# Latent attention heads in pairs, and the row minima of the next unit between the score tiles

## The chip, the cores and the metric

The kernel runs on one core of a Trainium2 chip. The metric is the device time of one execution in microseconds; the time of a kernel is the median of its runs. The engines are TensorE (PE, with its weight loads listed as PEld), VectorE (DVE), ScalarE (ACT), GpSimd (POOL) and SyncE (SP, which issues the DMAs).

## The reference

One layer of a hybrid encoder, 1024 tokens of width 1024, all in float32. The part that the change touches is the multi-head latent attention; beside it runs a banded attention of eight heads, and an output projection and a gated MLP with a short convolution follow.

```python
h = modulate(rmsnorm(x, g_attn_norm), sh_a, sc_a)
q_lat, kv_lat, k_rope, ca_qkv = split(h @ w_in)
q  = (rmsnorm(q_lat) @ w_q_up)  -> (S, 8 heads, 96)
kv = (rmsnorm(kv_lat) @ w_kv_up) -> k_nope (64), v (64) per head
k  = concat(k_nope, broadcast(k_rope))             # 96 per head
q, k = rmsnorm per head, rotary on the last 32
s = q k^T * 96**-0.5, masked: key chunk <= query chunk (chunks of 64)
o_mla = softmax(s) v
o_ca  = banded attention of 8 more heads
x = x + g_a * (concat(o_mla, o_ca) @ w_out)
x = x + g_m * (silu(gate) * val @ w_down)          # gate, val: conv of h @ w_up
```

## The kernel before, in words

The kernel is written as a sequence of operations on tiles of named pools; a planner at build time takes that sequence and fixes the order of each engine's queue from its own estimates. `tc.high_priority(offset=n)` moves a block's operations n places ahead in the planner's ranking (`OFF_S` = 400 for scores, `OFF_V` = 200 for values). `tc.issue_after(ins)` lets the block's operations on that engine stand only behind `ins`. A pool tag with `bufs=n` has n buffers; a new tile of that tag waits until the oldest one's readers are done. At run time each engine takes its queue in order.

Large matrix products are split into a high and a low half (fp32r), three matmuls for one.

The latent attention works in units: a unit (`Latent`) is one head and one group `g` of 512 queries; `gr` is the group of four heads, `hh` the head in it. Keys stand on partitions in the score tiles (scores transposed), queries along the columns. A unit of `g` = 0 has four key blocks and two score tiles, one of `g` = 1 has eight key blocks and four score tiles; the four blocks on the diagonal are shortened and masked by a memset. The steps of a unit:

- `prep`: two pages, `Q` and `K`, are made by `qk_page` (L612 and on): four transposes on TensorE into a PSUM buffer of tag `T` (one buffer, `TB` = 1), a copy to the high half on ScalarE (L619 for queries, L622 for keys), a difference to the low half on VectorE (L620, L623).
- `rows_min` (L724 to L738): for four tiles of 128 queries a one-pass product of high halves (`sm`, L732) in a score slot, a mask (L734), the minimum over the keys on VectorE (`mm`, L736), and its transpose into one row (`mtm`, L737, tag `T`). ScalarE copies the negated row into row 96 of the query page (L738), so that the score product subtracts it by itself. (Keys carry the negative scale, so the minimum is what a maximum usually is.)
- `scores(x)`: one tile `st` with up to two pieces of 512 columns (three matmuls each, L751 to L753), masks (L755), exponentials on ScalarE (`pm`, L761).
- `values(x)`: products of these with the values (`pvm`, L779). The value operand holds 64 columns of values and 64 of ones, so one half of the accumulator's partitions holds the output and the other half the sums; which half is which alternates with `hh`. After the last tile ScalarE copies the sums across (`om`, L787), VectorE takes the reciprocal (L788) and the product (L789), and SP stores 64 rows of `oT_d` (L790).

Both `sm` and `st` live in the PSUM tag `S`, which has two slots of two banks; the accumulator `pv` has one buffer.

The order: for each of the 16 units, in the order head by head with `g` = 0 then 1, `begin(next unit)` (its needs, `prep` and all of `rows_min`) comes ahead of this unit's score tiles, and the values lag two score tiles behind. `pace` puts in filler work: after each step it takes pieces from a list of generators (projections for later heads, then `f_up(0)` and `f_up(1)`, the up-projections of the two groups of four latent heads, then `f_oca`, the output projection of the banded heads) worth `R_MLA` = 0.5 times the step's cost. `need(key)` forces a generator to its end; a unit needs `up1` if `gr` or `g` is 1, otherwise `up0`. The tag `pg` (`pgtile`, six buffers of the size of a page) holds the transposed latents until `f_up(1)` has read them. Before the latent units the banded heads run in tiles (`Unit`, with scores in L656), and the first latent unit is begun at their end. After them the output projection of the latent heads (`op`) reads `oT_d` back by token tiles.

Of the kernel before, what the change touches and what calls it, by code (L numbers as in the profile page):

```python
# [12 lines left out]
F32 = mybir.dt.float32  # L13
F32R = mybir.dt.float32r
# [3 lines left out]
AF = mybir.ActivationFunctionType  # L18
ALU = mybir.AluOpType
AX = mybir.AxisListType  # L20
PSUM = bass.MemoryType.PSUM
MUL, ADD, SUB, MIN, MAX = ALU.mult, ALU.add, ALU.subtract, ALU.min, ALU.max

P = 128
D = 1024
S = 1024
# [5 lines left out]
BIG = 1e30  # L32
QR, KVR, ROPE, NOPE, VD = 256, 128, 32, 64, 64
QK = NOPE + ROPE
# [5 lines left out]
OFF_S, OFF_P, OFF_V = 400, 200, 200  # L40
# [22 lines left out]
def layer_kernel(ctx, tc, I, out):  # L63
    nc = tc.nc
    pe, act, dve, pool, sp = nc.tensor, nc.scalar, nc.vector, nc.gpsimd, nc.sync
# [18 lines left out]
    cst = ctx.enter_context(tc.tile_pool(name="cst", bufs=1))  # L84
    dram = ctx.enter_context(tc.tile_pool(name="dram", bufs=1, space=bass.MemoryType.DRAM))
    oT_d = dram.tile([ND, P, S], F32, name="oT_d")
# [9 lines left out]
    ident = cst.tile([P, P], F32, name="ident")  # L96
# [11 lines left out]
    gk_m = cst.tile([P, 1], F32, name="gk_m")  # L108
# [22 lines left out]
    ps = psA.__enter__()  # L131
# [12 lines left out]
    def pgtile(shape, dt, name):  # L144
        return apg.tile(shape, dt, name=name, tag="pg", bufs=6)
# [11 lines left out]
    trail = []  # L157
# [79 lines left out]
    for d in range(ND):  # L237
        if d + 1 < ND:
            load_ada(d + 1)
        w = wada[d]  # L240
# [91 lines left out]
    at = att.__enter__()  # L332
# [279 lines left out]
    def qk_page(src, name, rows, tag, bufs, gain, top=None):  # L612

        pt = ps.tile([P, 512], F32, name=f"{name}_ps", tag="T", bufs=TB)
        for j in range(4):
            pe.transpose(pt[:top or rows, j * P:(j + 1) * P], src(j), ident[:])
        pg = at.tile([P, 2, 512], F32R, name=name, tag=tag, bufs=bufs)
        if gain is None:
            act.activation(pg[:rows, 0], pt[:rows], AF.Copy)  # L619
            dve.tensor_tensor(pg[:rows, 1], pt[:rows], f32(pg[:rows, 0]), op=SUB)  # L620
        else:
            act.activation(pg[:top or rows, 0], pt[:top or rows], AF.Copy, scale=gain[:top or rows])  # L622
            dve.scalar_tensor_tensor(pg[:rows, 1], pt[:rows], gain[:rows], f32(pg[:rows, 0]), op0=MUL, op1=SUB)  # L623
        return pg

    class Unit:
# [58 lines left out]
        def values(u, i):  # L685
            if i % 4 == 0:
                u.pv = ps.tile([P, 512], F32, name=f"pv{u.nm}_{u.g}", tag="pv", bufs=1)
            c = slice((i % 4) * P, (i % 4 + 1) * P)
            tt, lo, nk = u.pt[i]
            todo = [(lo + j, tt[:, h * nk + j, :]) for j in range(nk) for h in range(2)]  # L690
            with tc.high_priority(offset=OFF_V):
                for x, (j, mov) in enumerate(todo):
                    last = pe.matmul(u.pv[:, c], u.vst(j), mov, start=(x == 0), stop=(x == len(todo) - 1))
                trail.append(last.ins)
                if i % 4 == 3:
                    dst = at.tile([P, 512], F32, name=f"o{u.nm}_{u.g}", tag="o", bufs=1)
                    r0, r1 = (slice(64, 128), slice(0, 64)) if u.odd else (slice(0, 64), slice(64, 128))
                    inv = vscale[u.vs][1]
                    act.activation(dst[r0], u.pv[r1], AF.Copy, scale=inv[r1])
                    dve.scalar_tensor_tensor(dst[r0], u.pv[r0], inv[r0], dst[r0], op0=MUL, op1=ADD)  # L700
                    sp.dma_start(u.dst_d[r0, u.g * 512:(u.g + 1) * 512], dst[r0])
            return 56 * len(todo)

    class Latent:


        def __init__(u, gr, hh, g):
            u.gr, u.hh, u.g, u.nm = gr, hh, g, f"m{gr}{hh}"
            u.need = ["up1"] if gr or g else ["up0"]
            d = [[(4 * g, 0)], [(4 * g + 1, 128), (4 * g + 3, 384)], [(4 * g + 2, 256)]]  # L710
            u.pieces = [[(kb, 0)] for kb in range(4 * g)] + d
            u.pr = {}

        def prep(u):
            gr, hh, g = u.gr, u.hh, u.g
            u.q = qk_page(lambda j: mq[gr, (4 * g + j) // 2][:, j % 2, hh, 0:QK], f"mq{gr}{hh}_{g}", QK, "Q", 2, None)
            k = qk_page(lambda j: mk[gr, (4 * g + j) // 2][:, j % 2, hh, :], f"mk{gr}{hh}_{g}", QK, "K", 3, gk_m[:],
                        QK + 1)
            pages[gr, hh, g] = k
            u.k = [pages[gr, hh, i] for i in range(g + 1)]  # L720

        def rows_min(u):

            with tc.high_priority(offset=OFF_S):  # L724
                mt = ps.tile([P, 512], F32, name=f"mt{u.nm}_{u.g}", tag="T", bufs=TB)
                for j in range(4):
                    n = (4 * u.g + j + 1) * P
                    nm = f"{u.nm}_{4 * u.g + j}"
                    s = ps.tile([P, 1024], F32, name=f"s{nm}", tag="S", bufs=2)
                    for c in range(0, n, 512):  # L730
                        w = min(512, n - c)
                        pe.matmul(s[:, c:c + w], u.q[:QK, 0, j * P:(j + 1) * P], u.k[c // 512][:QK, 0, :w],  # L732
                                  start=True, stop=True)
                    dve.memset(s[0:64, n - 64:n], BIG)  # L734
                    m = cst.tile([P, 1], F32, name=f"m{nm}", tag="m", bufs=4)
                    dve.tensor_reduce(m[:], s[:, :n], axis=AX.X, op=MIN)  # L736
                    last = pe.transpose(mt[0:1, j * P:(j + 1) * P], m[:], ident[:])  # L737
                act.activation(u.q[QK:QK + 1, 0], mt[0:1], AF.Copy, scale=-1.0)  # L738

        def scores(u, x):  # L740
# [25 lines left out]
        def values(u, x):  # L766
            if x == 0:
                u.pv = ps.tile([P, 512], F32, name=f"pv{u.nm}_{u.g}", tag="pv", bufs=1)
            cost = 0
            with tc.high_priority(offset=OFF_V):  # L770
                for y in (2 * x, 2 * x + 1):
                    if y >= len(u.pieces):
                        break
                    o = 0
                    for kb, c in u.pieces[y]:
                        w = 512 - c
                        o2 = u.hh % 2
                        v = mv[u.gr, kb][:, u.hh // 2, o2:o2 + 2, :].rearrange("p a b -> p (a b)")
                        last = pe.matmul(u.pv[:, c:], v, u.pr[y][:, o:o + w], start=(kb == 0),  # L779
                                         stop=(y == len(u.pieces) - 1))  # L780
                        o += w
                        cost += 4 * w / 2.4
                trail.append(last.ins)
                if 2 * x + 2 >= len(u.pieces):
                    dst = at.tile([P, 512], F32, name=f"o{u.nm}_{u.g}", tag="o", bufs=1)
                    r0, r1 = (slice(64, 128), slice(0, 64)) if u.hh % 2 else (slice(0, 64), slice(64, 128))
                    act.activation(dst[r0], u.pv[r1], AF.Copy)  # L787
                    dve.reciprocal(dst[r0], dst[r0])  # L788
                    dve.tensor_tensor(dst[r0], u.pv[r0], dst[r0], op=MUL)  # L789
                    sp.dma_start(oT_d[2 * u.gr + u.hh // 2][r0, u.g * 512:(u.g + 1) * 512], dst[r0])  # L790
            return cost

    biases = {}
# [59 lines left out]
    def pace(cost, ratio):  # L853
        debt[0] += cost * ratio
        while debt[0] > 0:
            c = fill_step()
            if c is None:
                debt[0] = 0.0
                return
            debt[0] -= c  # L860

    units = [ca_unit(p, g, o) for p in range(4) for g in range(2) for o in range(2)]
    lat = [Latent(gr, hh, g) for gr in range(2) for hh in range(4) for g in range(2)]

    def begin(u):
        need(u.need)
        u.prep()
        u.rows_min()

    tiles = [(u, i) for u in units for i in range(4 * u.g, 4 * u.g + 4)]  # L870
    for n in range(len(tiles) + DEPTH):
        if n < len(tiles):
            u, i = tiles[n]
            if i % 4 == 0:
                need(u.need)
                u.prep()
            pace(u.scores(i), R_CA)
        elif n == len(tiles):
            begin(lat[0])
        if n >= DEPTH:  # L880
            u, i = tiles[n - DEPTH]
            if i % 4 == 0:
                need(u.needv)
            pace(u.values(i), R_CA)
    wait = []
    for n, u in enumerate(lat):
        if n + 1 < len(lat):
            begin(lat[n + 1])
        for x in range(2 + 2 * u.g):
            pace(u.scores(x), R_MLA)  # L890
            wait.append((u, x))
            if len(wait) > 2:
                v, y = wait.pop(0)
                pace(v.values(y), R_MLA)
    for v, y in wait:
        v.values(y)
    need(["oca"])
# [322 lines left out]
```

## Time and profile before

| | us |
|---|---|
| median of 3 runs | 1573.38 (1569.08 to 1576.13) |
| the profiled execution | 1573.6 |
| its span, first to last instruction | 1571.8 |
| mean granted TensorE clock over the span | 0.917 |
| TensorE busy | 1366.2 (87% of the span) |
| VectorE busy | 1006.2 (64%) |
| ScalarE busy | 605.0 (38%) |
| GpSimd busy | 703.4 (45%) |

Busy time counts instructions of the engine itself; a busy TensorE is not TensorE at its peak, since the ends of pipelined matmuls are modelled and the granted clock can be below one. In the groups of instructions a row reads: line, engine, operation, output and input tiles, shapes and count, then busy time and mean duration in ns, then the idle time of that engine just ahead of these instructions and what ended most of it. A row of waits reads: the waiting engine and operation, the one that released it, total time, times, the longest. In the order of time a row gives start, duration, engine, line, operation, and in brackets the idle time ahead and its releaser. The span is also given in forty equal slices, each digit the busy share of a slice in tenths.

### The profile page before, as it was taken

What the parts mean: (1) busy time and instruction counts of PE and PEld (TensorE: products, weight loads), DVE (VectorE), ACT (ScalarE), POOL (GpSimd) and SP (SyncE); (2) the same over time, 40 slices, a digit from 0 to 9 for tenths busy, and PEclk for the clock granted to TensorE, in tenths of its full rate; (3) what the DMA queues carried; (4) which work ended last, traced back from release to release, by engine and by line L of the source; (5) the groups of instructions that cost most, each with busy time, mean ns of one, the idle gap of its engine ahead of it and who ended that gap; (6) DMA issues with size and microseconds to landing.
All of it is one profiled execution on the core that took longest, in us unless ns stands there. A gap on an engine that the chain in (4) does not pass through costs nothing.

```text
span 1571.8 us, 19114 instructions
## 1 busy us (share of the span) xinstructions
PE 1366.2 (87%) x6608; PEld 1090.8 (69%) x6608; DVE 1006.2 (64%) x1660; ACT 605.0 (38%) x1146; POOL 703.4 (45%) x643
## 2 busy tenths in 40 slices
PE   3869989998779787776789599999999999999997
PEld 2759868877546455544457488878788887787885
DVE  6865776665886334444346787777877777556653
ACT  5544443343554322223325443334444443333331
POOL 5264552564445000001037265556656664565662
PEclk9979969997888878778789699999999999999999
DMA  7323566454303100011173132232222234446542
GB/s 265 132 73 89 116 134 140 118 123 102 81 15 101 44 26 29 20 34 58 34 261 134 41 107 107 99 103 94 82 80 81 84 112 141 160 144 212 172 153 95
DMA packets 137821, 164.89 MB, mean 105 GB/s; under 512 B 71414, under 2 KB 102266, under 8 KB 136700
## 3 DMA queue, kind: packets, MB, share of 16 engines
q1 hardware_dynamic: 137724, 163.67, 34.5%
q8 instruction: 52, 0.85, 0.2%
q14 instruction: 45, 0.37, 0.1%
HBM read 119.07 MB, written 28.84 MB: 94 GB/s over the span
## 4 chain that ended last, share of the span: by engine, by line
PE 55%; DVE 15%; DMA 12%; POOL 8%; issue 6%; ACT 3%; SPq 1%; DVEq 0%; POOLq 0%; ACTq 0%
PE p L992 8%; PE p L994 8%; PE p L993 8%; PE pvm L779 4%; POOL wds L82 4%; DMA aw<-w_ada 4%; PE sc L656 3%; PE dnp L1135 2%; PE dnp L1137 2%; PE dnp L1136 2%; DVE om L788 2%; PE stm L751 2%; PE stm L752 1%; PE stm L753 1%; DVE adacc L244 1%
## 5 line engine op out<-in xcount | busy, mean ns | idle before, releaser
L82 POOL TENSOR_TENSOR wds<-wd,wds 128x512 fp32r<-128x512 f32 x88 | 152.7, 1755 | 102.2 <-ACT wds L75 102.2
L82 POOL TENSOR_TENSOR wc<-ws,wc 128x512 fp32r<-128x512 f32 x22 | 65.3, 2970 | 129.3 <-ACT wc L75 129.3
L1137 PE MATMUL dnp<-wds,g 128*128 128x512 f32 x308 | 119.4, 394 | 3.6 <-DVE g L82 3.6
L1135 PE MATMUL dnp<-wds,g 128*128 128x512 f32 x308 | 120.0, 392 | 1.7 <-DVE xo L1143 1.7
L1136 PE MATMUL dnp<-wds,g 128*128 128x512 f32 x308 | 120.4, 392 | 0.0
L1125 DVE TENSOR_TENSOR wd<-wd,gmbc 128x1024 f32<-128x1024 f32 x44 | 65.0, 1478 | 86.2 <-DMA wd<-w_down 86.2
L75 ACT ACTIVATE wds<-wd 128x512 fp32r<-128x512 f32 x88 | 54.8, 624 | 160.2 <-PE dnp L1137 152.6
L761 ACT ACTIVATE pm<-stm 128x512 f32<-128x512 f32 (+1 forms) x80 | 43.6, 551 | 123.6 <-DVE stm L755 67.2
L779 PE MATMUL pvm<-pm,vt 128*128 128x512 f32 (+1 forms) x192 | 80.6, 544 | 6.3 <-ACT pm L761 6.0
L755 DVE MEMSET stm<- 64x64 f32 x64 | 7.1, 112 | 120.9 <-PE stm L753 105.6
L71 POOL TENSOR_SCALAR hlc<-Pc,ric 128x640 f16<-128x640 f32 (+2 forms) x64 | 45.7, 716 | 81.2 <-DVE ric L676 41.4
L788 DVE RECIPROCAL om<-om 64x512 f32<-64x512 f32 x16 | 53.6, 3347 | 44.3 <-ACT om L787 44.2
L1069 DVE SCALAR_TENSOR_TENSOR u<-c,pk,u 128x1023 f32<-128x1023 f32 x44 | 77.6, 1769 | 1.8 <-ACT u L1068 1.8
L82 POOL TENSOR_TENSOR cl<-cl,ch 128x512 fp32r<-128x512 f32 x8 | 10.4, 1302 | 150.5 <-ACT ch L75 149.3
L82 DVE TENSOR_TENSOR g<-gr,g 128x512 fp32r<-128x512 f32 x44 | 70.4, 1602 | 11.4 <-ACT g L75 11.4
L656 PE MATMUL sc<-k,q 64*128 64x512 f32 (+3 forms) x288 | 70.5, 373 | 7.4 <-ACT Pc L673 5.5
L673 ACT ACTIVATE Pc<-sc,mc 128x640 f32<-128x640 f32 (+2 forms) x64 | 42.2, 659 | 86.3 <-DVE mc L670 57.1
L82 POOL TENSOR_TENSOR wa<-wu,wa 128x512 fp32r<-128x512 f32 x22 | 32.7, 1488 | 90.1 <-ACT wa L75 46.2
L1068 ACT ACTIVATE u<-c,pk 128x1024 f32<-128x1024 f32 x44 | 52.3, 1237 | 51.4 <-DVE c L1100 51.4
L429 DVE SCALAR_TENSOR_TENSOR aacc<-aw,cs,aacc 128x256 f32<-128x256 f32 x84 | 44.8, 533 | 42.2 <-DMA aw<-w_ada 42.0
L1104 ACT ACTIVATE u<-u 128x1024 f32<-128x1024 f32 x22 | 23.4, 1063 | 125.7 <-DVE u L1070 125.6
L1083 DVE TENSOR_TENSOR ws<-wu,wu 128x512 f32<-128x512 f32 x22 | 25.9, 1179 | 69.4 <-DMA wu<-w_up 69.4
(359 smaller groups left out, 4527.9 us busy)
## 6 DMA issues: line engine op xcount, KB each, us to landing
wu<-w_up SPq DMA_DIRECT2D x44, 512.0 KB, 4.3
wd<-w_down SPq DMA_DIRECT2D x44, 512.0 KB, 5.0
aw<-w_ada SPq DMA_DIRECT2D x96, 128.0 KB, 2.3
g_d<-u SPq DMA_DIRECT2D x22, 512.0 KB, 2.6
gr<-g_d SPq DMA_DIRECT2D x44, 256.0 KB, 3.5
x<-x SPq DMA_DIRECT2D x16, 512.0 KB, 6.1
adaw<-w_ada_a SPq DMA_DIRECT2D x8, 1024.0 KB, 5.5
wq_r<-w_qk SPq DMA_DIRECT2D x32, 128.0 KB, 2.8
```

The source lines that it names most:

```text
L82: (pool if eng == "p" else dve).tensor_tensor(o, i, f32(hi), op=SUB)
L656: last = pe.matmul(s[:, c:c + w], qpg[rs_, a, q], kpgs[kh][rs_, b, ko:ko + w], start=(a == 0 and b == 0), stop=(a == 1))
L779: last = pe.matmul(u.pv[:, c:], v, u.pr[y][:, o:o + w], start=(kb == 0), stop=(y == len(u.pieces) - 1))
L788: dve.reciprocal(dst[r0], dst[r0])
L992: pe.matmul(pt, sh, pg[:, 0], start=(k == 0), stop=False)
L993: pe.matmul(pt, sh, pg[:, 1], start=False, stop=False)
L994: pe.matmul(pt, sl, pg[:, 0], start=False, stop=(k == 3))
L1069: dve.scalar_tensor_tensor(u[:, 1:], c[:, :S - 1], pk[:, cv + 1:cv + 2], u[:, 1:], op0=MUL, op1=ADD)
L1125: dve.tensor_tensor(raw[:], raw[:], gmbc[:], op=MUL)
L1135: pe.matmul(pts[t][n], sh, w[n][:, 0], start=(j == 0), stop=False)
L1136: pe.matmul(pts[t][n], sh, w[n][:, 1], start=False, stop=False)
L1137: pe.matmul(pts[t][n], sl, w[n][:, 0], start=False, stop=(j == NF - 1))
```

## The change

The latent units come in pairs of heads: both heads of a pair for `g` = 0, then both for `g` = 1. After the last value tile ScalarE copies the sums (into `d`) and the values (into `o`) of a head out of the accumulator, each head to its half of two shared tiles; behind the second head of the pair VectorE takes the reciprocal of the shared sums in two pieces of 256 columns, and one product and one store serve both heads. The two tiles have two buffers.

`rows_min` is split. `row_min(j)` does one of the four tiles up to the minimum, and its four calls for the next unit stand between the score tiles of this one. `shift` does the four transposes, behind the last matmul recorded so far, and the copy of the row; it stands after this unit's last score tile. `begin` is now `need` and `prep` alone, and is called for the unit after the next, behind `shift`. Key pages of `g` = 1 come from the tag `pg`. The first unit's minima stand at the end of the banded heads as before, its `shift` and the second unit's `begin` after them.

```diff
-        pg = at.tile([P, 2, 512], F32R, name=name, tag=tag, bufs=bufs)
+        pg = pgtile([P, 2, 512], F32R, name) if tag == "pg" else at.tile([P, 2, 512], F32R, name=name, tag=tag, bufs=bufs)
...
-                    dst = at.tile([P, 512], F32, name=f"o{u.nm}_{u.g}", tag="o", bufs=1)
+                    dst = at.tile([P, 512], F32, name=f"o{u.nm}_{u.g}", tag="o", bufs=2)
...
-            k = qk_page(lambda j: mk[gr, (4 * g + j) // 2][:, j % 2, hh, :], f"mk{gr}{hh}_{g}", QK, "K", 3, gk_m[:],
-                        QK + 1)
+            k = qk_page(lambda j: mk[gr, (4 * g + j) // 2][:, j % 2, hh, :], f"mk{gr}{hh}_{g}", QK,
+                        "pg" if g else "K", 3, gk_m[:], QK + 1)
...
-        def rows_min(u):
+        def row_min(u, j):
+
+            with tc.high_priority(offset=OFF_S):
+                n = (4 * u.g + j + 1) * P
+                nm = f"{u.nm}_{4 * u.g + j}"
+                s = ps.tile([P, 1024], F32, name=f"s{nm}", tag="S", bufs=2)
+                for c in range(0, n, 512):
+                    w = min(512, n - c)
+                    pe.matmul(s[:, c:c + w], u.q[:QK, 0, j * P:(j + 1) * P], u.k[c // 512][:QK, 0, :w],
+                              start=True, stop=True)
+                dve.memset(s[0:64, n - 64:n], BIG)
+                m = cst.tile([P, 1], F32, name=f"m{nm}", tag="m", bufs=4)
+                dve.tensor_reduce(m[:], s[:, :n], axis=AX.X, op=MIN)
+                u.m.append(m)
+
+        def shift(u):
 
             with tc.high_priority(offset=OFF_S):
                 mt = ps.tile([P, 512], F32, name=f"mt{u.nm}_{u.g}", tag="T", bufs=TB)
...
+                with tc.issue_after(trail[-1]):
+                    for j in range(4):
+                        pe.transpose(mt[0:1, j * P:(j + 1) * P], u.m[j][:], ident[:])
                 act.activation(u.q[QK:QK + 1, 0], mt[0:1], AF.Copy, scale=-1.0)
...
-                    dst = at.tile([P, 512], F32, name=f"o{u.nm}_{u.g}", tag="o", bufs=1)
+                    if u.hh % 2 == 0:
+                        u.out = [at.tile([P, 512], F32, name=f"{i}{u.nm}_{u.g}", tag="o", bufs=2) for i in "os"]
+                        outs[u.gr, u.hh, u.g] = u.out
+                    else:
+                        u.out = outs[u.gr, u.hh - 1, u.g]
+                    o, d = u.out
                     r0, r1 = (slice(64, 128), slice(0, 64)) if u.hh % 2 else (slice(0, 64), slice(64, 128))
-                    act.activation(dst[r0], u.pv[r1], AF.Copy)
-                    dve.reciprocal(dst[r0], dst[r0])
-                    dve.tensor_tensor(dst[r0], u.pv[r0], dst[r0], op=MUL)
-                    sp.dma_start(oT_d[2 * u.gr + u.hh // 2][r0, u.g * 512:(u.g + 1) * 512], dst[r0])
+                    act.activation(d[r0], u.pv[r1], AF.Copy)
+                    act.activation(o[r0], u.pv[r0], AF.Copy)
+            if u.hh % 2 and 2 * x + 2 >= len(u.pieces):
+                for c in range(0, 512, 256):
+                    dve.reciprocal(d[:, c:c + 256], d[:, c:c + 256])
+                dve.tensor_tensor(o[:], o[:], d[:], op=MUL)
+                sp.dma_start(oT_d[2 * u.gr + u.hh // 2][:, u.g * 512:(u.g + 1) * 512], o[:])
...
-    lat = [Latent(gr, hh, g) for gr in range(2) for hh in range(4) for g in range(2)]
+    lat = [Latent(gr, hh + i, g) for gr in range(2) for hh in (0, 2) for g in range(2) for i in range(2)]
...
         u.prep()
-        u.rows_min()
...
             begin(lat[0])
+            for j in range(4):
+                lat[0].row_min(j)
...
+    lat[0].shift()
+    begin(lat[1])
     wait = []
     for n, u in enumerate(lat):
-        if n + 1 < len(lat):
-            begin(lat[n + 1])
-        for x in range(2 + 2 * u.g):
+        nx = 2 + 2 * u.g
+        for x in range(nx):
             pace(u.scores(x), R_MLA)
+            if n + 1 < len(lat):
+                for j in range(4 * x // nx, 4 * (x + 1) // nx):
+                    lat[n + 1].row_min(j)
             wait.append((u, x))
             if len(wait) > 2:
                 v, y = wait.pop(0)
                 pace(v.values(y), R_MLA)
+        if n + 1 < len(lat):
+            lat[n + 1].shift()
+        if n + 2 < len(lat):
+            begin(lat[n + 2])
```

More of the change, by code (lines that the diff above doesn't have):

```diff
@@ L702, in values @@
             return 56 * len(todo)
+    outs = {}
     class Latent:
@@ L711, in __init__ @@
             u.pieces = [[(kb, 0)] for kb in range(4 * g)] + d
-            u.pr = {}
+            u.pr, u.m = {}, []
         def prep(u):
@@ L724, in rows_min @@
+        def shift(u):
             with tc.high_priority(offset=OFF_S):
                 mt = ps.tile([P, 512], F32, name=f"mt{u.nm}_{u.g}", tag="T", bufs=TB)
[L726 to L737, printed above, removed]
+                with tc.issue_after(trail[-1]):
+                    for j in range(4):
+                        pe.transpose(mt[0:1, j * P:(j + 1) * P], u.m[j][:], ident[:])
```

## The prediction

> **What bounds the kernel now.** I read the page from the top: busy shares, the span in slices, the costliest groups; then the busy time by stages, then what ended TensorE's waits in the stage of the latent heads, and last the order of time around one such wait.
>
> ```profile
> span 1571.8 us, 19114 instructions
> PE 1366.2 (87%) x6608; PEld 1090.8 (69%) x6608; DVE 1006.2 (64%) x1660; ACT 605.0 (38%) x1146; POOL 703.4 (45%) x643
> PE   3869989998779787776789599999999999999997
> PEclk9979969997888878778789699999999999999999
> L788 DVE RECIPROCAL om<-om 64x512 f32<-64x512 f32 x16 | 53.6, 3347 | 44.3 <-ACT om L787 44.2
> ```
>
> The profiled execution took 1573.6 us, 1.8 us outside its span; the runs shown have the median 1573.38 (1569.08 to 1576.13), so the sum below, made against 1573.6, holds against the median as well. TensorE is the busiest engine, but from the twelfth to the twentieth slice it is at seven or eight tenths, and its granted clock is low there too. The stage rows give the sizes. Their columns are the stretch, its length, the busy time of PE, PEld, DVE, ACT and POOL with instruction counts, the granted clock, the DMA share and GB/s.
>
> ```profile
> 100.00:380.00 280.00, 263.01 (x1852) 230.84 (x1851) 176.02 (x518) 113.26 (x303) 130.68 (x197) 0.91 0.51 115
> 455.00:515.00 60.00, 50.41 (x211) 35.24 (x209) 40.04 (x99) 30.16 (x62) 25.84 (x25) 0.91 0.23 75
> 515.00:803.00 288.00, 212.13 (x763) 141.79 (x764) 118.89 (x205) 81.90 (x146) 15.16 (x12) 0.79 0.13 40
> 450.00:803.00 353.00, 266.68 (x991) 180.00 (x992) 163.92 (x320) 115.05 (x215) 41.00 (x37) 0.82 0.14 45
> ...
> 510.00:515.00 5.00, 4.12 (x24) 3.18 (x22) 1.46 (x3) 2.27 (x4) 0.00 (x0) 1.00 0.30 101
> 515.00:520.00 5.00, 0.57 (x4) 0.41 (x4) 4.83 (x7) 1.21 (x2) 1.27 (x1) 0.72 0.01 4
> 520.00:525.00 5.00, 4.80 (x13) 3.19 (x13) 1.58 (x5) 1.33 (x3) 0.00 (x0) 0.50 0.11 26
> ```
>
> From 450 to 803 us, the stage of the sixteen latent units, TensorE is idle for 353.0 - 266.7 = 86.3 us, and what it does it does at 0.82 of its clock. Busy time times clock, 266.7 x 0.82 = 218.7 us, is the stage's work at full clock: 134 us of this stage are idleness and slow clock. No other engine is near full (DVE 164 of 353). The stage of the banded heads (100 to 380) runs the same engines with 6% idle. The short rows show how the two losses hang together: where TensorE stands for 4.4 of 5 us, the next row is at half clock.
>
> ```profile
> PE mtm L737 <- DVE mm L736: 45.5, 14, 5.3
> PE sm L732 <- ACT mk L622: 14.8, 13, 2.2
> PE pvm L779 <- ACT pm L761: 6.0, 4, 2.4
> PE sm L732 <- ACT mq L619: 2.5, 3, 1.1
> ...
> 562.31 0.69 ACT L622 ACTIVATE mk<-mk_ps,gk_m 97x512 fp32r<-97x512 f32 x1
> 562.32 3.35 DVE L788 RECIPROCAL om<-om 64x512 f32<-64x512 f32 x1 [2.05 <-ACT om L787]
> 563.05 0.49 PE L732 MATMUL sm<-mk,mq 96*128 96x128 f32 x2 [0.96 <-ACT mk L622]
> 565.59 0.64 DVE L623 SCALAR_TENSOR_TENSOR mk<-mk_ps,gk_m,mk 96x512 fp32r<-96x512 f32 x1
> 566.31 0.19 DVE L734 MEMSET sm<- 64x64 f32 x2
> 566.41 0.67 DVE L789 TENSOR_TENSOR om<-pvm,om 64x512 f32<-64x512 f32 x1
> 567.00 0.60 DVE L736 TENSOR_REDUCE mm<-sm 128x1 f32<-128x128 f32 x2
> 567.42 0.37 PE L737 MATMUL mtm<-ident,mm 128*1 128x128 f32 x1 [3.87 <-DVE mm L736]
> 570.70 0.60 ACT L761 ACTIVATE pm<-stm 128x512 f32<-128x512 f32 x1 [7.70 <-PE stm L753]
> ```
>
> The wait rows give total, times and longest: of the 86.3 us, 45.5 are TensorE's transposes of the minima waiting for the reduction on VectorE, 14.8 + 2.5 are the first score rows of a unit waiting for its key or query page. The order of time says why the first is so long. At the start of a unit the next unit's first two minimum tiles are multiplied (563.05); they fill both score slots in PSUM; VectorE has just begun the previous unit's reciprocal, 3.35 us, so mask and reduction come at 566 to 567; the transpose sits at the head of TensorE's queue and everything behind it stands. ScalarE idles 7.7 us.
>
> **The change part by part**, with these durations.
>
> ```profile
> L787 ACT ACTIVATE om<-pvm 64x512 f32<-64x512 f32 x16 | 9.5, 591 | 22.3 <-PE pvm L779 22.2
> L789 DVE TENSOR_TENSOR om<-pvm,om 64x512 f32<-64x512 f32 x16 | 10.9, 681 | 0.3
> L82 DVE TENSOR_TENSOR wo<-wor,wo 128x512 fp32r<-128x512 f32 x4 | 2.7, 686 | 0.2
> L736 DVE TENSOR_REDUCE mm<-sm 128x1 f32<-128x1024 f32 x8 | 9.8, 1222 | 0.2
> L738 ACT ACTIVATE mq<-mtm 1x512 fp32r<-1x512 f32 x15 | 8.8, 584 | 2.2 <-PE mtm L737 2.0
> L737 PE MATMUL mtm<-ident,mm 128*1 128x128 f32 x59 | 22.0, 377 | 45.5 <-DVE mm L736 45.5
> ...
> 579.68 1.88 PE L779 MATMUL pvm<-pm,vt 128*128 128x512 f32 x4
> 510.04 0.60 PE L616 MATMUL mq_ps<-ident,qn 128*96 128x128 f32 x4
> 513.52 0.60 PE L616 MATMUL mk_ps<-ident,kn 128*97 128x128 f32 x4
> ...
> L619 ACT ACTIVATE mq<-mq_ps 96x512 fp32r<-96x512 f32 x14 | 8.2, 588 | 24.2 <-PE stm L753 24.2
> L620 DVE TENSOR_TENSOR mq<-mq_ps,mq 96x512 fp32r<-96x512 f32 x14 | 9.6, 685 | 8.6 <-ACT mq L619 8.6
> L622 ACT ACTIVATE mk<-mk_ps,gk_m 97x512 fp32r<-97x512 f32 x14 | 9.6, 683 | 1.5 <-PE mk_ps L616 1.2
> L790 SPq DMA_DIRECT2D oT_d<-om x16: 445/452/467, 472.0 to 802.5; - x16
> ```
>
> Minima. Their 64 transposes move behind the last scores and the value matmuls that follow these. The last reduction (1.22 us, before it a mask of 0.1) then runs under about 1.9 us of value matmuls, and nothing queues behind a transpose that is not ready. The 45.5 us go; I take 0 left. Ends: 0 and 45.5.
>
> Pages. A unit's pages are now begun a unit earlier, after the row of its predecessor is in place; but both pages and that row share one PSUM buffer, and the unit's first minimum tile follows the next score tile. Chain: two times 0.60 us of transposes, 0.59 + 0.69 for the query page, 0.68 for the key page, about 3.2 us, under one score tile and two value tiles, about as long. I leave half of 17.3: 8.6. Ends: 0 and 17.3.
>
> The new serial step. Between units now stand four transposes and the copy of the row (0.58), before the next unit's first scores: 4 x 0.38 + 0.58 + 0.2 of handing over = 2.3 us, at 15 boundaries 34 us if nothing fills it. What fills it are the two value tiles that lag behind, ready by then. I take 0.5 us each, 7.5. Ends: 0 and 34.
>
> Reciprocals. The trace has no 128x256 one. Partitions do not set a VectorE operation's time here (0.681 us on 64 partitions, 0.686 on 128 of the same 512 columns), so one lasts half of 3.35, 1.67 us, and the eight pairs of heads take 26.8 us where 53.6 stood; the other end, time by element, would be 53.6 again. A pair can still hold up masks and pages behind it, 3.35 us at eight places. It comes due behind the second score tile of the next unit, where masked tiles or the next pages follow, but no reduction stands at the head of TensorE's queue any more. I take half, 4 x 3.35 = 13.4. Ends: 0 and 26.8.
>
> Eviction. ScalarE gets 16 more copies of 0.59, 9.5 us, on an engine busy for 115 of 353; VectorE's products fall from 16 x 0.68 to 8 x 0.69. The accumulator is free after two copies instead of after copy, reciprocal and product, some 3.4 us earlier. Eight stores of twice the size replace sixteen, so SP issues 8 x 0.45 us less. After the very last unit copy, two reciprocals and product follow each other as today, 0.59 + 3.35 + 0.69; the projection of the first token tiles covers it as it does today. All together 0; ends -6 (the accumulator waits of row L779) and +1.
>
> Order of units and the second group's up-projection. The up-projection must now be issued before the third unit rather than the second. Its work is the same; 0, ends -4 and +4, the size of its longest wait, 4.4 us:
>
> ```profile
> PE qu L151 <- ACT uqr L556: 4.4, 1, 4.4
> ```
>
> Sum of idleness: 86.3 - 45.5 - 17.3 = 23.5 stay, + 8.6 + 7.5 + 13.4 = 53.0 us.
>
> Clock. In 515 to 803 half clock was granted for 288 x 2 x 0.21 = 121 us. Spread over the 14 waits on minima that is 8.6 us of half clock each. I count six stalls of that size as left (half of the reciprocal pairs and two others): 52 us of a stage of about 290, clock 1 - 52/580 = 0.91, the value of both neighbouring stages; I take 0.90. The stage becomes 218.7/0.90 + 53.0 = 296 us instead of 353: 57 us less, 1573.6 - 57 = 1516.6, forecast 1516. All low ends with a clock of 0.95: 218.7/0.95 + 23.5 - 10 = 244, which is 1465. All high ends with today's clock, the wait on minima apart (if it stayed, nothing else would be new): 266.7 + 23.5 + 17.3 + 34 + 26.8 + 5 = 373, which is 1594.
>
> The rows 515 to 525 went to half clock when TensorE had stood for 4.4 of 5 us. [...]
>
> The row 510 to 515 holds eight page transposes (the two rows of 0.60 us above) at a clock of 1.00. [...]
>
> **Rivals.**
>
> Full clock: if stalls shorter than today's never lower the clock, the stage takes 218.7 + 53 = 272, the time 1492. For it: the interior of a unit, without stalls, is at 1.00 in the rows. Against: the 0.91 of the stage of banded heads, which stalls little. Chance 0.17. [...]
>
> The wait changes its name: the planner places minimum tiles in front of values, and they wait for the one buffer of row and pages, or hold a score slot. Idleness 23.5 + 17.3 + 34 + 13.4 = 88, clock 0.82: 355, no change (1575). Half of it: 1546. For it: today's queue already holds a transpose against 3.9 us of nothing, so the planned order does not know the real waits. Against: these operations now have other work beside them. Chance 0.14, a third of it within 0.5%.
>
> [...] Chance 0.05. [...]
>
> Slower: VectorE takes the reciprocal pair ahead of the query page's low half. Then the PSUM buffer comes free 3.35 us late, the key page and the first minimum tile with it: 3.35 + 0.69 + 0.60 + 0.68 = 5.3 us per pair, against 45.5/14 = 3.3 now, and the row of 2.3 us uncovered at each boundary: the sum of the high ends, 1594. It decides from about 86 us of idleness. For it: 562.32 shows VectorE taking the reciprocal first. Against: it is half as frequent. Chance 0.11.
>
> **How the numbers follow.** The forecast's own case, 1495 to 1540, has 0.53, full clock 0.17, changed name 0.14, cold boundaries 0.05, slower 0.11. Measurements of this kernel tell 0.5%, some 8 us, from no change. Faster: 0.53 + 0.17 + 0.09 + 0.05 = 0.84; same 0.05; slower 0.11. The range 1470 to 1570 leaves out the slower case, the worst of the changed name and the lowest ends.
>
> **What would show it.** Right: waits of the minimum transposes for VectorE under 10 us; the stage some 296 us long at a clock of 0.90 with about 53 us idle; sixteen reciprocals of 128x256 near 1.67 us; no more 7 us holes in ScalarE's exponentials. Wrong: TensorE's minimum rows waiting for pages by more than 17 us; transposes waiting over 2 us per boundary; reciprocals of 3.3 us; a clock still near 0.82 although the holes are gone; or time lost outside the stage, at the projection that follows.

## The result, and the profile after

The changed kernel takes 1519.17 us, median of 3 runs (1509.05 to 1521.31), against 1573.38: the ratio is 0.9642, 95% interval 0.9566 to 0.9717. Run again later, beside the experiments, it gave 1519.27 and the ratio 0.9668 (0.9643 to 0.9693). The forecast was 1516, in a range of 1470 to 1570.

The page of the changed kernel, its head:

```profile
span 1517.5 us, 19050 instructions
PE 1348.7 (89%) x6608; PEld 1081.6 (71%) x6608; DVE 973.8 (64%) x1652; ACT 615.1 (41%) x1162; POOL 705.0 (46%) x643
```

Where the time went is told by stages: the kernel before first, from 450 us to the last value product, and the rest; then the same two of the changed kernel. Columns as in the prediction.

```profile
450.00:797.00 347.00, 262.63 (x980) 177.37 (x981) 159.87 (x318) 113.21 (x212) 39.72 (x36) 0.82 0.13 42
797.00:1571.00 774.00, 731.07 (x3168) 594.21 (x3166) 539.38 (x474) 294.23 (x444) 442.03 (x277) 0.97 0.37 124
```

```profile
450.00:741.00 291.00, 245.82 (x952) 167.28 (x951) 126.95 (x294) 117.17 (x217) 37.27 (x35) 0.88 0.13 46
741.00:1517.00 776.00, 729.28 (x3170) 591.85 (x3168) 536.47 (x475) 296.12 (x447) 445.51 (x279) 0.97 0.35 125
```

All of it is in the latent stage: 347 us became 291, and what follows is as long as before (774 and 776 us). TensorE's idle time there fell from 347.0 - 262.6 = 84.4 to 291.0 - 245.8 = 45.2 us, by 39 us. Its busy time fell by 17 us for the same work: busy time times clock is 262.6 x 0.82 = 215 and 245.8 x 0.88 = 216, so these 17 us are the higher clock.

What TensorE waits for in the changed kernel, from 450 to 748 us (total, times, longest), and the new operations of the eviction:

```profile
PE stm L759 <- ACT mq L746: 15.9, 15, 1.9
PE mtm L745 <- DVE mm L736: 7.8, 11, 2.7
PE mk_ps L616 <- DVE mq L620: 5.2, 3, 2.3
PE sm L732 <- ACT pm L769: 3.9, 10, 0.9
PE stm L759 <- ACT pm L769: 3.5, 10, 0.5
...
L804 DVE RECIPROCAL sm<-sm 128x256 f32<-128x256 f32 x16 | 26.9, 1720 | 6.7 <-ACT sm L800 6.7
L800 ACT ACTIVATE sm<-pvm 64x512 f32<-64x512 f32 x16 | 9.5, 592 | 17.2 <-PE pvm L787 17.1
L801 ACT ACTIVATE om<-pvm 64x512 f32<-64x512 f32 x16 | 9.5, 592 | 0.4
```

The 45.5 us of minimum transposes waiting for VectorE are 7.8 us, and the waits of minimum rows for key pages fell from 14.8 to 1.2 us, too few for the head of the list. The first place is new: the first scores of a unit wait for the copy of the row of minima, at each of the 15 boundaries. The order of time at one of them, in chosen lines, shows what makes it long.

```profile
595.42 1.57 PE L787 MATMUL pvm<-pm,vt 128*128 128x384 f32 x6
596.83 0.27 PE L745 MATMUL mtm<-ident,mm 128*1 128x128 f32 x1
597.03 0.59 ACT L800 ACTIVATE sm<-pvm 64x512 f32<-64x512 f32 x1 [1.66 <-PE pvm L787]
597.64 0.59 ACT L801 ACTIVATE om<-pvm 64x512 f32<-64x512 f32 x1
597.65 3.36 DVE L804 RECIPROCAL sm<-sm 128x256 f32<-128x256 f32 x2 [1.35 <-ACT sm L800]
598.26 0.58 ACT L746 ACTIVATE mq<-mtm 1x512 fp32r<-1x512 f32 x1
598.89 0.50 PE L759 MATMUL stm<-mq,mk 97*128 97x512 f32 x1 [1.79 <-ACT mq L746]
```

The transposed row is ready at 597.1 (596.83 + 0.27). ScalarE first does the two accumulator copies, which the change put there, and only then the row: TensorE stands for 1.79 us.

### The profile page after: what moved, and what is told of

It is laid out like the page before. It is cut to its first block, busy times and chain, and to the rows that moved or that the text cites. A ratio compares the mean times of both kernels' runs of the same rounds, so it can differ in the third digit from the quotient of the medians.

```text
span 1517.5 us, 19050 instructions
## 1 busy us (share of the span) xinstructions
PE 1348.7 (89%) x6608; PEld 1081.6 (71%) x6608; DVE 973.8 (64%) x1652; ACT 615.1 (41%) x1162; POOL 705.0 (46%) x643
## 4 chain that ended last, share of the span: by engine, by line
PE 63%; DVE 14%; DMA 10%; ACT 4%; issue 4%; POOL 4%; SPq 1%; DVEq 0%; ACTq 0%; POOLq 0%
PE p L1017 8%; PE p L1019 8%; PE p L1018 7%; PE dnp L1162 4%; PE dnp L1160 4%; PE dnp L1161 4%; PE pvm L787 4%; DMA aw<-w_ada 4%; PE sc L656 2%; PE stm L759 2%; DVE adacc L244 2%; PE stm L760 1%; PE ipv L151 1%; PE stm L761 1%; PE ipv L153 1%
## 5 line engine op out<-in xcount | busy, mean ns | idle before, releaser
L787 PE MATMUL pvm<-pm,vt 128*128 128x512 f32 (+1 forms) x192 | 84.6, 547 | 1.0 <-ACT pm L769 0.9
L1162 PEld LDWEIGHTS dnp<-wds,g 128*128 128x128 f32 x308 | 57.8, 188 | 15.7 <-DVE g L82 3.8
L1160 PEld LDWEIGHTS dnp<-wds,g 128*128 128x128 f32 x308 | 57.8, 188 | 15.0 <-DVE xo L1168 2.7
L759 PE MATMUL stm<-mq,mk 97*128 97x512 f32 (+3 forms) x96 | 49.0, 513 | 21.1 <-ACT mq L746 15.9
L1161 PEld LDWEIGHTS dnp<-wds,g 128*128 128x128 f32 x308 | 57.8, 188 | 12.0
```

The source lines that it names most:

```text
L759: pe.matmul(s[:, o:o + w], kp[:QK + 1, 0, ks], u.q[:QK + 1, 0, c:], start=True, stop=False)
L1160: pe.matmul(pts[t][n], sh, w[n][:, 0], start=(j == 0), stop=False)
L1161: pe.matmul(pts[t][n], sh, w[n][:, 1], start=False, stop=False)
L1162: pe.matmul(pts[t][n], sl, w[n][:, 0], start=False, stop=(j == NF - 1))
```

## The experiments

Every experiment was run beside the kernel before, and what is compared is the ratio to it, with its 95% interval. The experiments ran in three batches, on three chips; the changed kernel was repeated only in the last one, so runs of different batches are compared through their ratios.

**Pairs alone.** The eviction in pairs, the minima as before.

```diff
         need(u.need)
         u.prep()
+        u.rows_min()
...
-    lat[0].shift()
-    begin(lat[1])
```

> The pairs and the shared reciprocal of the change, with the minima as before (all four ahead of the previous unit's scores, each transpose right behind its minimum). Theory (the stall is the transpose at the head of TensorE's queue, and a reciprocal of 3.35 us on VectorE makes it long): a pair of reciprocals still stands there at every second boundary, so the waits on minima fall from 45.5 to about 25 us, the clock rises little, and the time is about 1545. Rival (the reciprocals alone are the loss, and halving them gives nearly all): about 1525. Rival (the reciprocals do not matter, only the place of the minima): 1565 to 1575.

1551.21 us, ratio 0.9855 (0.9826 to 0.9885). Its waits:

```profile
PE mtm L739 <- DVE mm L738: 24.6, 13, 3.8
PE sm L734 <- ACT mk L622: 16.1, 11, 2.2
```

That is nearly what the theory said (25 us, 1545): with reciprocals at every second boundary, about half of the wait is gone.

**Minima alone.** The changed kernel with the eviction of before, a reciprocal for each head, but with two buffers for its tile. The units stay in the new order, in pairs of heads.

```diff
-                    act.activation(d[r0], u.pv[r1], AF.Copy)
-                    act.activation(o[r0], u.pv[r0], AF.Copy)
...
+                    act.activation(dst[r0], u.pv[r1], AF.Copy)
+                    dve.reciprocal(dst[r0], dst[r0])
+                    dve.tensor_tensor(dst[r0], u.pv[r0], dst[r0], op=MUL)
+                    sp.dma_start(oT_d[2 * u.gr + u.hh // 2][r0, u.g * 512:(u.g + 1) * 512], dst[r0])
```

> The change with the eviction of before in it: every head has its own reciprocal of 64x512 (3.35 us, sixteen of them) and its own store; order of units and place of the minima as changed. Theory (minima no longer hold TensorE's queue, but a reciprocal still delays masks, pages and the accumulator): some 10 to 20 us above the changed kernel's 1519, so 1530 to 1540. Rival (with the minima moved, reciprocals are hidden): 1515 to 1523. Rival (the eviction is the larger part of the gain): 1550 or more.

1517.25 us, ratio 0.9643 (0.9618 to 0.9667): as fast as the whole change. The theory's 1530 to 1540 fell; the rival's figure came out, though not its reason, as the run without reciprocals will show. In its waits the row costs less (10.7 us, 15.9 in the changed kernel) and the exponentials more (12.7, 3.5); the last line is its stage, to the last value product:

```profile
PE stm L759 <- ACT pm L769: 12.7, 14, 2.4
PE stm L759 <- ACT mq L746: 10.7, 14, 1.2
PE mtm L745 <- DVE mm L736: 9.3, 12, 3.2
...
450.00:736.00 286.00, 238.56 (x954) 162.77 (x954) 160.79 (x305) 110.38 (x205) 38.22 (x35) 0.91 0.15 47
```

**The kernel before without its reciprocals.** It leaves out the sixteen reciprocals, so its output is not the layer's.

```diff
-                    dve.reciprocal(dst[r0], dst[r0])
```

> The kernel before with the sixteen reciprocals left out (the output is multiplied by the sums instead of divided), order of the program the same. Theory (the reciprocal in front of the minima makes the stall): waits on minima fall from 45.5 us to 10 to 15, idle time of the stage from 86 to about 50, the clock rises to 0.86 or more, the time is about 1530. Rival (the stall is that of bunched minima and two score slots, whatever VectorE does): waits above 30 us, time above 1555.

1531.55 us, ratio 0.9735 (0.9712 to 0.9759), and the wait on minima is

```profile
PE mtm L737 <- DVE mm L736: 16.0, 13, 1.9
PE sm L732 <- ACT mk L622: 15.0, 13, 3.2
```

So the reciprocal made about two thirds of that wait, 45.5 to 16.0 us, close to the theory's 10 to 15; but moving the minima (1517 us) gains more than taking every reciprocal away (1532 us).

**Minima bunched.** The changed kernel with the next unit's four minimum tiles ahead of this unit's scores; the transposes stay behind the last scores.

```diff
         nx = 2 + 2 * u.g
+        if n + 1 < len(lat):
+            for j in range(4):
+                lat[n + 1].row_min(j)
         for x in range(nx):
             pace(u.scores(x), R_MLA)
-            if n + 1 < len(lat):
-                for j in range(4 * x // nx, 4 * (x + 1) // nx):
-                    lat[n + 1].row_min(j)
```

> The change, but with the four minimum tiles of the next unit all ahead of this unit's score tiles (as before), their transposes still behind the last scores. Theory (a transpose at the head of the queue was the loss): within 8 us of the changed kernel, 1515 to 1528. Rival (minimum tiles in both score slots hold back the first scores, so the place between the score tiles matters): 1535 to 1550, with TensorE's minimum rows and first scores waiting for VectorE's reductions.

1560.43 us, ratio 0.9911 (0.9884 to 0.9938), slower even than the rival's 1535 to 1550. Its waits and its stage:

```profile
PE sm L732 <- DVE mm L736: 22.6, 11, 3.8
PE sm L732 <- ACT mk L622: 18.2, 12, 2.3
PE sm L732 <- ACT mq L619: 8.1, 5, 4.4
PE mtm L745 <- DVE mm L736: 1.4, 1, 1.4
...
450.00:780.00 330.00, 263.17 (x950) 177.97 (x950) 121.79 (x284) 115.97 (x215) 38.37 (x34) 0.82 0.12 40
```

The transposes no longer wait (1.4 us), and it does not help: the third minimum tile waits instead, for a score slot that the first one's reduction holds, and pages are waited for more than before (18.2 + 8.1 us, 14.8 + 2.5 before), since the tiles ask for pages that have just been begun. So the gain comes from the place of the tiles between the scores; how much of it is the slots and how much the pages, this run does not separate. Moving the transposes without it gives nothing: pairs alone, with the transposes in their old place, took 1551.

**The changed kernel without its reciprocals.** It leaves them out in the same way.

```diff
-                for c in range(0, 512, 256):
-                    dve.reciprocal(d[:, c:c + 256], d[:, c:c + 256])
```

> The changed kernel with its sixteen 128x256 reciprocals left out (outputs are multiplied by the sums). The prediction left 13.4 us of idleness to them, with half clock some 25 us. Theory after the second experiment (minima alone gave 1517 with sixteen long reciprocals in it): reciprocals are hidden, 1512 to 1522. Rival (they still delay the query page's low half, and through the one PSUM buffer the key page): waits of the key page's transposes for VectorE fall from 5.2 us to near 0 and the time to 1495 to 1508.

1507.95 us, ratio 0.9597 (0.9574 to 0.962): 11 us below the changed kernel, at the rival's upper end. The wait of the key page's transposes for the query page's low half, 5.2 us, is gone from the list. So the reciprocals in pairs are not hidden. Then minima alone, with twice the reciprocal time, should have been slower and was not. One explanation is that its single copy on ScalarE lets the row through earlier (10.7 us of waits, not 15.9); the next two runs test that.

**The row ahead of the accumulator copies**, in ScalarE's queue. `rowc[-1]` is the row copy of the next unit.

```diff
-                act.activation(u.q[QK:QK + 1, 0], mt[0:1], AF.Copy, scale=-1.0)
+                rowc.append(act.activation(u.q[QK:QK + 1, 0], mt[0:1], AF.Copy, scale=-1.0).ins)
...
+                    with tc.issue_after(rowc[-1]):
+                        act.activation(d[r0], u.pv[r1], AF.Copy)
+                        act.activation(o[r0], u.pv[r0], AF.Copy)
```

> The changed kernel; ScalarE copies the negated row of minima ahead of the two accumulator copies of the unit before (which now stand behind it in ScalarE's queue). Theory (of the 15.9 us that first scores wait for the row, about 0.67 us each, 10 us in all, is the copy itself, the rest the accumulator copies ahead of it): waits for the row 10 us, time 1510 to 1516. Rival (the accumulator then comes free later and the values wait instead): 1519 to 1530.

1514.21 us, ratio 0.9621 (0.9589 to 0.9653). That overlaps the changed kernel's interval (0.9643 to 0.9693): unclear. The wait for the row falls to the 10 us expected, and another grows from 5.2 to 10.2; the last line is its stage:

```profile
PE mk_ps L616 <- DVE mq L620: 10.2, 3, 3.4
PE stm L760 <- ACT mq L747: 10.0, 14, 1.3
...
450.00:735.00 285.00, 241.98 (x953) 164.62 (x953) 127.96 (x294) 117.25 (x218) 37.47 (x35) 0.90 0.14 47
```

**The second copy on VectorE.**

```diff
-                    act.activation(o[r0], u.pv[r0], AF.Copy)
+                    dve.tensor_copy(o[r0], u.pv[r0])
```

> The changed kernel with the copy of the values out of the accumulator on VectorE instead of ScalarE (0.68 us each). Theory (the copies ahead of the row on ScalarE cost its waits): waits for the row fall from 15.9 to about 12 us, time 1512 to 1518. Rival (VectorE, with the reciprocals, delays masks and reductions as much): 1519 to 1526.

1507.33 us, ratio 0.9599 (0.9578 to 0.962), clear of the changed kernel (0.9643 to 0.9693 beside the last experiments) and below what the theory said. The waits, and the stage:

```profile
PE stm L759 <- ACT mq L746: 10.1, 12, 1.4
PE mk_ps L616 <- DVE mq L620: 9.1, 3, 3.1
...
450.00:731.00 281.00, 235.78 (x958) 161.69 (x957) 139.83 (x311) 110.05 (x205) 38.67 (x35) 0.91 0.14 47
```

So the extra copy on ScalarE, which the prediction costed at nothing, costs some 12 us there. That it does so by holding up the row is not shown. The row ahead of the copies takes the same 6 us off that wait, and its ratio can be told neither from this run's nor from the changed kernel's. And here TensorE's idle time in the stage did not fall at all: 281.0 - 235.8 = 45.2 us, as in the changed kernel, since other waits grew. The stage is 10 us shorter because the same work (235.8 x 0.91 = 215) ran at a clock of 0.91 instead of 0.88. Why the clock is higher with as much idleness stays open.

The kernel with one copy and long reciprocals (minima alone) is as fast as the one with two copies and short ones, so the shorter reciprocals seem to give about as much as that copy takes. This is inferred from the three runs; the two evictions differ in more than that.

**Heads in turn.** Minima alone, with the units in the order of before.

```diff
-    lat = [Latent(gr, hh + i, g) for gr in range(2) for hh in (0, 2) for g in range(2) for i in range(2)]
+    lat = [Latent(gr, hh, g) for gr in range(2) for hh in range(4) for g in range(2)]
```

> The second experiment (minima moved, every head its own eviction), with the units in the order of before, head by head. Theory (the pairing of heads gives nothing once the minima are moved): 1512 to 1524. Rival (the order of units helps, since the second group's up-projection is needed later): 1526 to 1540.

1524.48 us, ratio 0.9703 (0.9684 to 0.9723) against 0.9643 (0.9618 to 0.9667) in the other order: between the two expectations. The order of units is worth about 0.6%. Its stage:

```profile
450.00:751.00 301.00, 253.46 (x963) 171.39 (x964) 162.65 (x312) 109.86 (x206) 39.42 (x35) 0.87 0.14 45
```

It is idle as long as minima alone (301.0 - 253.5 = 47.5 us, 286.0 - 238.6 = 47.4), at a clock of 0.87 instead of 0.91. Why the order changes the clock is open; the rival's reason, the later up-projection, is not shown.

**The changed kernel again**, as a yardstick for the three that follow.

> The changed kernel unchanged, as the yardstick of this chip and day for the next ones: 1510 to 1521, ratio 0.960 to 0.967.

1519.27 us (1514.63 to 1524.36), ratio 0.9668 (0.9643 to 0.9693).

**A PSUM buffer of the key page's own**: its transposes go to the filler's tag `mm`.

```diff
-        pt = ps.tile([P, 512], F32, name=f"{name}_ps", tag="T", bufs=TB)
+        pt = ps.tile([P, 512], F32, name=f"{name}_ps", tag=pst, bufs=psb)
...
-                        "pg" if g else "K", 3, gk_m[:], QK + 1)
+                        "pg" if g else "K", 3, gk_m[:], QK + 1, "mm", 2)
```

> The changed kernel with the key page's transposes in one of the two PSUM buffers of the filler's tag instead of the single buffer T that query page and row of minima use. Theory (one buffer for three: the key page's transposes wait for the query page's low half, 5.2 us, and these stalls bring half clock): no such wait, 4 to 10 us less than the yardstick. Rival (the filler's products then lack a buffer): equal or up to 8 us more.

1517.73 us, ratio 0.966 (0.9629 to 0.969): no difference from the changed kernel beside it. The key page's wait of 5.2 us is gone, and the filler waited once for 6.0 us (0.6 in the changed kernel); why it did is open:

```profile
PE oc L151 <- ACT ch L75: 6.0, 1, 6.0
```

**Idle products.** Five matmuls that nothing reads, behind the four transposes.

```diff
-                        pe.transpose(mt[0:1, j * P:(j + 1) * P], u.m[j][:], ident[:])
+                        last = pe.transpose(mt[0:1, j * P:(j + 1) * P], u.m[j][:], ident[:])
                 act.activation(u.q[QK:QK + 1, 0], mt[0:1], AF.Copy, scale=-1.0)
+                dm = ps.tile([P, 512], F32, name=f"dm{u.nm}_{u.g}", tag="mm", bufs=2)
+                with tc.issue_after(last.ins):
+                    for j in range(5):
+                        pe.matmul(dm[:], u.k[0][:QK, 0, 0:P], u.k[0][:QK, 0, :], start=(j == 0), stop=(j == 4))
```

> The changed kernel with five idle products of 512 columns (0.23 us each at full clock, never read) behind the four transposes at each of 15 boundaries, 17 us of TensorE work in all, where the first scores wait for the row. Theory (these short stalls still bring half clock, so filling them pays for the work): granted clock of the latent stage 0.93 or more against 0.87 to 0.90, time within 6 us of the yardstick. Rival (the clock does not depend on stalls this short): clock unchanged, time 8 to 17 us above the yardstick.

1510.32 us, ratio 0.9607 (0.9585 to 0.9628) against 0.9668 (0.9643 to 0.9693): 9 us faster with an estimated 17 us more work. Its stage, to the last value product, and its wait for the row:

```profile
450.00:729.00 279.00, 242.78 (x1027) 168.94 (x1027) 128.58 (x293) 117.11 (x217) 37.16 (x34) 0.95 0.14 48
...
PE stm L763 <- ACT mq L746: 1.9, 3, 0.7
```

The clock went to 0.95, the wait for the row from 15.9 to 1.9 us. The waits of the minimum transposes grew (13.8 us), and the time fell all the same, further than expected. Busy time times clock is 242.8 x 0.95 = 231 us, some 15 more than the 216 before, which is the added work; TensorE was yet busy for 3 us less, and idle for 36 us, not 45. The planner also put other operations in another order, so the 9 us are not all shown to be the clock's; that the stage ran at the higher clock with this work in it, 0.95 against 0.88, is.

**The copy on VectorE and the key page's buffer together.**

> The copy of the values on VectorE and the key page's own PSUM buffer together. Theory (two separate waits): 1497 to 1507, the lowest so far. Rival (one wait behind the other): as the copy on VectorE alone, 1505 to 1513.

1506.39 us, ratio 0.9603 (0.9574 to 0.9633): not to be told from the copy on VectorE alone, and within both expectations, which overlap; so the question is open. These two, and the idle products, are the fastest versions seen that keep the reciprocals; the copy together with the idle products was not run.

## Why the prediction was right, point by point

The reading was right: the loss was TensorE's idleness at the unit boundaries and the half clock behind it, and the change removed both in part. Stage 298 us (450 to 748) where 296 was said, idle 298.0 - 250.6 = 47 us where 53 was said, clock 0.87 where 0.90 was said and 0.82 stood before:

```profile
450.00:748.00 298.00, 250.56 (x965) 170.23 (x964) 131.01 (x297) 119.61 (x221) 39.54 (x37) 0.87 0.15 50
```

ScalarE's exponentials, which had stood for up to 9.9 us before, now stand for at most 5.4 in the stage, and no wait of a minimum transpose is above 2.7 us. (The busy tenths that the prediction reads as seven or eight have a nine in the thirteenth slice and a six in the nineteenth; nothing hangs on it.)

The terms are less good than their sum, and that the sum came within 2 us is in part luck. TensorE was idle for 6 us less than said and, at the lower clock, busy for 8 us more (250.6, against 218.7/0.90 = 243). Within the idleness, minima and serial step took 16 us more than said; what was left to everything else but the pages, 23.5 + 13.4 = 36.9 us, was 17.3.

- Minima: 0 us left was said, 7.8 measured. The reason given was that nothing queues any more behind a transpose that is not ready. Bunched minima show that this alone is not enough: with the transposes out of the way, TensorE waited for the score slots (22.6 us) and the pages (26.3 us) instead. The place of the tiles between the scores carries the term.
- Pages: 8.6 said. Minimum rows wait 1.2 us for key pages; the single PSUM buffer shows as 5.2 us between query and key page, 6.4 in all. Giving the key page a buffer of its own gained nothing, but another wait came with it, so what the 5.2 us are worth is open.
- The serial step: 7.5 said, 15.9 measured, twice as much. With the row ahead of the copies it is 10.0, so 5.9 us of it are the accumulator copies ahead of it, the sixteen of before and the sixteen new ones. The step that failed is "Eviction ... All together 0", with an upper end of +1: the new copies were set against ScalarE's total of 115 busy us in 353, and their place in its queue, just ahead of the row, was not looked at. Taking the new ones off ScalarE is worth some 12 us. That gain shows in the clock and not in idle time, and by what path is open.
- Reciprocals: 1.67 us said, 1.72 measured, 26.9 in all. 13.4 us of idleness were said, some 25 us with the half clock behind it; without them the kernel is 11 us faster, so the term was about twice too large. Halving them gave nothing net, it seems because the pairing brought the extra copies.
- Order of units: 0 said, ends -4 and +4; about 0.6%, some 9 us of gain, measured, with the eviction of before.
- Clock: six stalls of today's size were counted for half clock. In fact no stall of that size is left: the longest of the stage is 2.7 us, against 5.3 before. The clock is low behind the short ones all the same: in the six us from the start of the row copy it is 0.50 to 0.72 at 11 of the 15 boundaries, and 1.00 at the other four. Reckoned as in the prediction, half clock lasted 2 x 0.13 x 298 = 77 us where 52 were said.

Of the rivals, full clock (1492) did not come, nor the slower one. The wait that changes its name is what bunched minima do, at 1560. The case of the cold boundaries, with its chance of 0.05, no run shows as such; measured are the low clock behind 11 of the 15 boundaries and a time of 1519.

## What to carry to other kernels

When two kinds of tile share two buffers, look at the order in which they take them: a batch of preparatory tiles ahead of the real work holds the buffers until another engine has read them (22.6 us of waits with the minima bunched), and spreading them between the real tiles can be worth more than making that engine faster (1517 us here, against 1532 without any reciprocal). A copy on an engine with much idle time need not be free (some 12 us here, on a ScalarE busy for 117 of 291): look at what stands behind it in that engine's queue, not at the engine's total. Test a combined change in its parts: here the minima with the new order of units gave all of the gain, and the shared eviction gave and took back about the same.

## What the runs showed of the hardware

In the changed kernel half clock came behind stalls much shorter than the long ones of the kernel before, which were of up to 5.3 us. From 613 to 620 us, no stall of TensorE was longer than 1.2 us. The three longest, and the rows of five us:

```profile
613.74 0.50 PE L732 MATMUL sm<-mk,mq 96*128 96x512 f32 x1 [0.66 <-ACT pm L769]
616.63 0.50 PE L759 MATMUL stm<-mq,mk 97*128 97x512 f32 x1 [1.16 <-ACT mq L746]
618.48 0.69 PE L759 MATMUL stm<-mq,mk 97*128 97x384 f32 x1 [0.45 <-ACT pm L769]
...
615.00:620.00 5.00, 3.19 (x12) 2.50 (x13) 1.04 (x4) 2.61 (x5) 0.00 (x0) 0.80 0.00 0
620.00:625.00 5.00, 4.59 (x13) 3.00 (x12) 1.46 (x5) 1.28 (x2) 0.00 (x0) 0.50 0.00 0
```

In rows of one us the clock stands at 1.00 from 610 to 617 us, at 0.98 in the next and at 0.50 from 618: it fell with TensorE busy for 2.75 of the five us before (613 to 618). No long stall is among these: three short ones, of 0.66, 0.43 and 1.16 us, are the 2.25 us of idleness. Work put at the boundaries paid for itself here: an estimated 17 us of idle products went with a kernel 9 us faster, and with a clock of 0.95 in the stage instead of 0.88. The estimate is 75 times 0.23 us, the step from one matmul of 512 columns to the next at a clock of 1.00 in the changed kernel (0.22 to 0.24 us from 611 to 612 us). And the reciprocal's time went by its columns, not its partitions: 3.35 us for 64x512, 1.72 us for 128x256.
